# First guess of the norm roots on ScalarE, with the activation tables requested ahead

## The chip, the cores and the metric

One core of one Trainium2 chip runs the whole program. The metric is device microseconds of one execution, as the median of the runs shown.

## The reference, cut to what matters

Four layers work on 256 latent and 256 context tokens of width 1024 (512 columns). Layers 0 and 3 mix tokens by windowed attention with grouped keys, layer 1 by latent attention (MLA), layer 2 by a gated linear recurrence; each is followed by a gated MLP with a short convolution. Norms stand everywhere:

```python
def rmsnorm(x, gain):
    y = x * lax.rsqrt(jnp.mean(x * x, axis=-1, keepdims=True) + EPS)
    return y * gain

for layer in range(DEPTH):
    h = modulate(rmsnorm(x, norm1[layer]), sh1, sc1)      # latent, and context in the same way
    x = x + g1 * mixer(h)       # queries and keys: rmsnorm per head; MLA: also its two low-rank vectors
    x = x + g2 * conv_ffn(modulate(rmsnorm(x, norm2[layer]), sh2, sc2))
```

The root 1 / sqrt(mean + EPS) is what the change computes in another way.

## The kernel before, in words

The residual stream X lies transposed in SBUF: eight tiles of 128 features by 512 tokens, columns 0 to 255 context and 256 to 511 latent. Weights come in units of 128 x 1024 floats (`load`, L215), are split by ScalarE into a rounded high part (`convert`, L222) and by GpSimd into the rest (L226), and every product of a weight matrix takes three matmuls (`mm3`, L235 to L237).

A residual norm is the class `Norm`. `squares` (L434, L436) squares X on ScalarE and sums the tiles on VectorE; `rsq` (L444) sums over features by matmuls with a column of ones into a bank of PSUM, takes the root there with `psum_rsqrt` (L292 to L299), and spreads it over the features with four matmuls (L448); `apply` (L458 to L465) writes the high and low parts of the normed tile. There are 15 such roots, of 128 x 2 values each: two in front of layer 0, two in each of the other six tails of a mixer or MLP that serve both streams, and one in the last layer, whose context half isn't needed. In a tail (`out_tail`) the context half of the last columns is finished first, and the root of the context runs while TensorE goes on with latent columns.

The roots of heads use `mean_rsqrt` (L286, then `rsqrt`, L276 to L281) on small SBUF tiles: one for the keys of each window-attention layer (L643), one for each of 12 blocks of queries (`q_post`, L690, with a scale at L691), two for the low-rank vectors of MLA (L840), two for its first group of heads (L972, L978) and twelve for the later groups (L990). Keys are multiplied by their root (L650, L883, L884), some rotated (L617, L622), copied (L655), and transposed on TensorE (L660, L888); in MLA the query root is folded into the scale of the scores (L920).

So `rsqrt` is twelve VectorE instructions one behind the other: mean plus epsilon, shift and subtract for the integer guess, and three Newton steps of three. `psum_rsqrt` is thirteen, with the guess in PSUM.

A framework traces the program, plans each engine's order of instructions from priorities (program order) and modelled durations, and places the semaphores; `tc.issue_after(x)` keeps what is traced inside it behind x on the same engine. Each engine then runs its own list in order. ScalarE's tables are loaded in sets; before, every load is placed where a function is missing from the set that is loaded. Silu (L185, L1197, L1224), Exp (L1002, L716, L727, L948, L1084), Sqrt (L1088) and Gelu (L1119) need sets; Copy, Identity and Square run under any.

Of the kernel before, what the change touches and what calls it, by code (L numbers as in the profile page):

```python
# [10 lines left out]
F32 = mybir.dt.float32  # L11
F32R = mybir.dt.float32r
BF16 = mybir.dt.bfloat16
I32 = mybir.dt.int32
AF = mybir.ActivationFunctionType
ALU = mybir.AluOpType
# [18 lines left out]
MAGIC = float(0x5F3759DF)  # L35
# [76 lines left out]
def hybrid_kernel(ctx: ExitStack, tc: tile.TileContext, xT, cc, ccT, W, modwa, modwb, modw, colv, rowv, tabs, band, out, depth=DEPTH, dbg=None):  # L112
# [67 lines left out]
    ones = const.tile([128, 1], F32, name="ones")  # L180
    condT = const.tile([128, KT, 32], F32, name="condT")
# [3 lines left out]
    nc.scalar.activation(condT, condT, AF.Silu)  # L185
# [25 lines left out]
    ident = tab("ident")  # L211
    def load(key):
        off, w = offs[key]
        raw = raw_p.tile([128, 1024], F32, tag="raw", name="raw")[:, :w]
        nc.sync.dma_start(raw, bass.AP(tensor=W.tensor, offset=W.offset + off, ap=[[w, 128], [1, w]]))  # L215
        return raw
# [55 lines left out]
    def rsqrt(v, n, steps=3):  # L272
        i = small(n, "rs_i", I32)
        y = small(n, "rs_y")
        t = small(n, "rs_t")
        nc.vector.tensor_scalar(i, v.bitcast(I32), 1, None, op0=ALU.logical_shift_right)  # L276
        nc.vector.tensor_scalar(y.bitcast(I32), i, -1.0, MAGIC, op0=ALU.mult, op1=ALU.add)
        for _ in range(steps):
            nc.vector.tensor_tensor(t, y, y, op=ALU.mult)
            nc.vector.scalar_tensor_tensor(t, t, -0.5, v, op0=ALU.mult, op1=ALU.mult)  # L280
            nc.vector.scalar_tensor_tensor(y, t, 1.5, y, op0=ALU.add, op1=ALU.mult)  # L281
        return y

    def mean_rsqrt(src, n, dim):
        v = small(n, "rs_v")
        nc.vector.tensor_scalar(v, src, 1.0 / dim, EPS, op0=ALU.mult, op1=ALU.add)  # L286
        return rsqrt(v, n)

    def psum_rsqrt(ps, n, dim):
        src, v2, i, y = (ps[:, a * n:(a + 1) * n] for a in range(4))  # L290
        v, t, r = small(n, "rs_v"), small(n, "rs_t"), small(n, "rs_y")
        nc.vector.tensor_scalar(v2, src, 1.0 / dim, EPS, op0=ALU.mult, op1=ALU.add)  # L292
        nc.vector.tensor_scalar(i.bitcast(I32), v2.bitcast(I32), 1, None, op0=ALU.logical_shift_right)
        nc.vector.tensor_scalar(y.bitcast(I32), i.bitcast(I32), -1.0, MAGIC, op0=ALU.mult, op1=ALU.add)
        nc.vector.tensor_scalar(v, src, 1.0 / dim, EPS, op0=ALU.mult, op1=ALU.add)
        for z in range(3):
            nc.vector.tensor_tensor(t, y, v, op=ALU.mult)
            nc.vector.scalar_tensor_tensor(t, t, -0.5, y, op0=ALU.mult, op1=ALU.mult)
            nc.vector.scalar_tensor_tensor(r if z == 2 else y, t, 1.5, y, op0=ALU.add, op1=ALU.mult)  # L299
        return r  # L300
# [109 lines left out]
    class Norm:  # L410
# [28 lines left out]
        def rsq(self, sums):  # L439
# [5 lines left out]
            rs = psum_rsqrt(ps, 2, D)  # L445
# [131 lines left out]
    def swa(l, i, q0, nm, nxt, first=None):  # L577
# [65 lines left out]
        rk = mean_rsqrt(ssk, 16, 64)  # L643
# [21 lines left out]
        def q_post(p, b, ps):  # L665
# [24 lines left out]
            rq = mean_rsqrt(ss, 8, 64)  # L690
            nc.vector.tensor_scalar(rqs[p][:, b * 8:(b + 1) * 8], rq, 0.125, None, op0=ALU.mult)  # L691
# [92 lines left out]
    def mla(l, nm, nxt):  # L784
# [16 lines left out]
        for c, w, ks in ((0, 288, (3, 3, 2)), (1, 384, (2, 2, 2, 2))):  # L801
# [38 lines left out]
            nc.vector.tensor_copy(rrs[c], mean_rsqrt(ss, 4, (256, 384)[c]))  # L840
# [131 lines left out]
        rk = mean_rsqrt(ss, 16, 96)  # L972
# [5 lines left out]
        q_scale(0, 0, 4, mean_rsqrt(ss, 16, 96))  # L978
        units = {}
        for hg in range(4):  # L980
            if hg < 3:
                group(hg + 1)
            for h in range(4):
                core(hg, h // 2, h % 2)
                core(hg, h // 2, 2 + h % 2)
                for b in MP[h] if hg < 3 else ():
# [3 lines left out]
                    rr = mean_rsqrt(ss, 8, 96)  # L990
# [30 lines left out]
    def lru(l, nm, nxt, rates):  # L1021
# [89 lines left out]
        def gelus(n, root):  # L1111
# [5 lines left out]
            with tc.issue_after(root):  # L1117
                for z in range(2):
                    nc.scalar.activation(gg[n][z], gps[2 * n + z], AF.Gelu_apprx_tanh)  # L1119
# [28 lines left out]
        gelus(3, roots[3])  # L1148
# [4 lines left out]
    def ffn(l, t0, nm, nxt):  # L1153
# [26 lines left out]
        def up(f, gh, gl, q):  # L1180
# [16 lines left out]
            nc.scalar.activation(y[:, t0:], y[:, t0:], AF.Silu)  # L1197
# [45 lines left out]

    nm = Norm(0, 0, 0)
# [173 lines left out]
```

## Time and profile before

| | us |
|---|---|
| median of 3 runs | 2228.76 (2225.44 to 2229.73) |
| the profiled execution | 2225.85 |
| its span, first to last instruction | 2224.0 |
| mean granted TensorE clock | 0.983 of full speed |
| table loads in the profile | 20 |

The rows name engines as PE (TensorE matmuls), PEld (its weight loads), DVE (VectorE), ACT (ScalarE), POOL (GpSimd) and SP (the queue that issues transfers). Times count from the first instruction. L and a number is a line of the kernel. Line 269 and line 270 are a helper that splits a tile into high and low part.

### The profile page before, as it was taken

What the parts mean: (1) busy time and instruction counts of PE and PEld (TensorE: products, weight loads), DVE (VectorE), ACT (ScalarE), POOL (GpSimd) and SP (SyncE); (2) the same over time, 40 slices, a digit from 0 to 9 for tenths busy, and PEclk for the clock granted to TensorE, in tenths of its full rate; (3) what the DMA queues carried; (4) which work ended last, traced back from release to release, by engine and by line L of the source; (5) the groups of instructions that cost most, each with busy time, mean ns of one, the idle gap of its engine ahead of it and who ended that gap; (6) DMA issues with size and microseconds to landing.
All of it is one profiled execution on the core that took longest, in us unless ns stands there. A gap on an engine that the chain in (4) does not pass through costs nothing.

```text
span 2224.0 us, 32888 instructions
## 1 busy us (share of the span) xinstructions
PE 2122.6 (95%) x12084; PEld 1764.6 (79%) x12084; DVE 1549.0 (70%) x3341; ACT 1037.4 (47%) x1860; POOL 1050.3 (47%) x760
## 2 busy tenths in 40 slices
PE   6999999999999999999999999889999999898999
PEld 4666888888888666878888887678888888678999
DVE  4677779777776886687888677857954456785333
ACT  4467553232346775532233376824332324675544
POOL 3331255544544113455455457654544444526887
PEclk9999999999999999999999999999999999999999
DMA  7534145554532011255555422224655552313665
GB/s 300 199 127 131 39 135 179 172 178 157 180 114 68 21 30 55 60 190 178 174 186 181 132 67 87 94 88 131 194 184 163 177 163 86 105 33 114 187 182 160
DMA packets 83888, 300.14 MB, mean 135 GB/s; under 512 B 11152, under 2 KB 12816, under 8 KB 81296
## 3 DMA queue, kind: packets, MB, share of 16 engines
q1 hardware_dynamic: 83728, 298.05, 41.9%
q8 instruction: 95, 1.56, 0.3%
q14 instruction: 65, 0.53, 0.1%
HBM read 296.97 MB, written 1.05 MB: 134 GB/s over the span
## 4 chain that ended last, share of the span: by engine, by line
PE 78%; DVE 13%; ACT 4%; DMA 2%; issue 1%; POOL 1%; SPq 0%; ACTq 0%; DVEq 0%
PE fl L235 8%; PE fl L236 8%; PE fl L237 8%; PE mm L236 7%; PE mm L237 7%; PE mm L235 7%; PE mo L235 4%; PE mo L236 4%; PE mo L237 4%; PE tp L235 3%; PE tp L236 3%; PE tp L237 3%; PE mo L751 2%; PE mm L938 2%; PE tp L745 2%
## 5 line engine op out<-in xcount | busy, mean ns | idle before, releaser
L226 POOL TENSOR_TENSOR wlo<-raw,whi 128x256 fp32r<-128x256 f32 (+3 forms) x709 | 1015.6, 1455 | 1106.4 <-ACT whi L222 1068.9
L222 ACT ACTIVATE whi<-raw 128x1024 fp32r<-128x1024 f32 (+3 forms) x367 | 382.5, 1043 | 493.0 <-PE tp L236 208.0
L397 DVE SCALAR_TENSOR_TENSOR junk<-mw,cbc 128x1024 bf16<-128x1024 f32 x256 | 463.8, 1812 | 28.6 <-DMA mw<-in_modw_dram 15.0
L237 PE MATMUL fl<-h_hi,wlo 128*128 128x512 f32 (+1 forms) x800 | 287.1, 359 | 0.1
L235 PE MATMUL fl<-h_hi,whi 128*128 128x512 f32 (+1 forms) x800 | 286.7, 358 | 0.0
L236 PE MATMUL fl<-h_lo,whi 128*128 128x512 f32 (+1 forms) x800 | 286.3, 358 | 0.0
L236 PE MATMUL mm<-h_lo,whi 128*128 128x512 f32 (+1 forms) x784 | 274.6, 352 | 2.5 <-POOL h_lo L463 1.1
L235 PE MATMUL mm<-h_hi,whi 128*128 128x512 f32 (+1 forms) x784 | 273.3, 350 | 2.5 <-ACT h_hi L459 2.5
L237 PE MATMUL mm<-h_hi,wlo 128*128 128x512 f32 (+1 forms) x784 | 273.1, 349 | 0.0
L1193 DVE SCALAR_TENSOR_TENSOR conv<-mm,colt,conv 128x510 f32<-128x510 f32 (+1 forms) x88 | 59.8, 679 | 188.9 <-ACT conv L1191 188.9
L1197 ACT ACTIVATE conv<-conv 128x512 f32<-128x512 f32 (+1 forms) x88 | 51.0, 580 | 291.1 <-DVE conv L1195 291.0
L237 PEld LDWEIGHTS fl<-h_hi,wlo 128*128 128x128 f32 x800 | 151.3, 189 | 23.2 <-POOL wlo L226 1.4
L236 PEld LDWEIGHTS fl<-h_lo,whi 128*128 128x128 f32 x800 | 151.3, 189 | 21.7
L235 PEld LDWEIGHTS fl<-h_hi,whi 128*128 128x128 f32 x800 | 151.5, 189 | 21.5
L236 PEld LDWEIGHTS mm<-h_lo,whi 128*128 128x128 f32 x784 | 148.2, 189 | 24.6 <-DVE h_lo L465 2.9
L235 PEld LDWEIGHTS mm<-h_hi,whi 128*128 128x128 f32 x784 | 148.6, 190 | 22.2 <-ACT h_hi L459 3.5
L237 PEld LDWEIGHTS mm<-h_hi,wlo 128*128 128x128 f32 x784 | 148.3, 189 | 18.8
L235 PE MATMUL mo<-g_hi,whi 128*128 128x512 f32 (+1 forms) x388 | 135.0, 348 | 8.3 <-DVE x L471 8.2
L471 DVE SCALAR_TENSOR_TENSOR x<-mo,modc,x 128x256 f32<-128x256 f32 x193 | 86.5, 476 | 76.5 <-PE mo L237 76.4
L237 PE MATMUL mo<-g_hi,wlo 128*128 128x512 f32 (+1 forms) x388 | 134.8, 347 | 0.0
L236 PE MATMUL mo<-g_lo,whi 128*128 128x512 f32 (+1 forms) x388 | 134.7, 347 | 0.0
L235 PE MATMUL tp<-g_hi,whi 128*128 128x512 f32 (+1 forms) x352 | 124.7, 354 | 0.0
(356 smaller groups left out, 4452.8 us busy)
## 6 DMA issues: line engine op xcount, KB each, us to landing
raw<-in_W_dram SPq DMA_DIRECT2D x352, 512.0 KB, 3.6
mw<-in_modw_dram SPq DMA_DIRECT2D x144, 512.0 KB, 4.2
mw<-in_modwa_dram SPq DMA_DIRECT2D x8, 1024.0 KB, 16.0
mw<-in_modwb_dram SPq DMA_DIRECT2D x16, 512.0 KB, 4.5
mw<-in_modwb_dram SPq DMA_DIRECT2D x8, 1024.0 KB, 9.4
cbc<-in_cc_dram SPq DMA_DIRECT2D x3, 1024.0 KB, 6.7
raw<-in_W_dram SPq DMA_DIRECT2D x8, 384.0 KB, 3.1
x<-in_xT_dram SPq DMA_DIRECT2D x8, 256.0 KB, 4.1
```

Source lines behind the costliest of these rows:

```text
L222: nc.scalar.activation(hi, raw, AF.Copy)
L226: nc.gpsimd.tensor_tensor(lo[:, cs], raw[:, cs], f32(hi[:, cs]), op=ALU.subtract)
L235: nc.tensor.matmul(ps, ah, bh, start=start and i == 0, stop=False, **kw)
L236: nc.tensor.matmul(ps, ah, bl, start=False, stop=False, **kw)
L237: op = nc.tensor.matmul(ps, al, bh, start=False, stop=stop and i == n - 1, **kw)
L397: nc.vector.scalar_tensor_tensor(junk, raw, 1.0, cbc[:, s], op0=ALU.mult, op1=ALU.mult, accum_out=modc[l][:, s, m:m + 1])
L471: nc.vector.scalar_tensor_tensor(X[m][:, half], ps[:, half], modc[l][:, s, part + m:part + m + 1], X[m][:, half], op0=ALU.mult, op1=ALU.add)
L745: nc.tensor.transpose(pp[:, c:c + 128], P[z][:, (2 * kp + kk) * 128:(2 * kp + kk + 1) * 128], ident)
L751: nc.tensor.matmul(po[r], v[0][:, kb, p * 128 + 64 * z:p * 128 + 64 * z + 64], pt[:, kp, (kk * 2 + z) * 128:(kk * 2 + z + 1) * 128], start ...
L938: nc.tensor.matmul(ps[:, c], d["q"][:96, 2 * hp + z, bc], d["k"][:96, 2 * hp + z, :nk], start=True, stop=True)
L1193: op = nc.vector.scalar_tensor_tensor(y3[:, :, 1:], g3[:, :, :255], cw[:, l, 0, f:f + 1], y3[:, :, 1:], op0=ALU.mult, op1=ALU.add)
L1197: nc.scalar.activation(y[:, t0:], y[:, t0:], AF.Silu)
```

## The change

The integer guess goes, and so do two of the three Newton steps. ScalarE computes e = Ln(c * (sum / dim + EPS)) with c = 2^-44, and y = Exp(-e / 2 + ln(c) / 2), which is the first guess; one Newton step follows on VectorE. Constants for the two biases lie in a small tile `seed`. For the queries of window attention the factor of an eighth goes into the second bias, so that the separate scale (L691) falls away, as does the copy of L840. One set holds both Ln and Exp; it is requested by an instruction of its own behind the first Silu of the program, behind the last Silu of each MLP but the final one, and behind the last Gelu of the recurrence, and Ln and Exp are kept behind that request.

```diff
@@ -32,7 +32,7 @@
 MP = ((), (0,), (1,), (2, 3))
 PP0, PP3 = (2, 4, 6), (2, 4, 6)
 QP0, QP3 = (0, 0, 1, 2), (0, 1)
-MAGIC = float(0x5F3759DF)
+LN_C = 2.0 ** -44
 
 
 def unit_plan():
@@ -178,11 +178,15 @@
     rowt = const.tile([128, NROWS], F32, name="rowt")
     tabt = const.tile([128, NTABS], F32, name="tabt")
     ones = const.tile([128, 1], F32, name="ones")
+    seed = const.tile([128, 3], F32, name="seed")
+    tables = [None]
+    for c, value in enumerate((LN_C * EPS, 0.5 * np.log(LN_C), 0.5 * np.log(LN_C) - np.log(8.0))):
+        nc.vector.memset(seed[:, c:c + 1], float(value))
     condT = const.tile([128, KT, 32], F32, name="condT")
     nc.gpsimd.memset(condT, 0.0)
     for j in range(2):
         nc.sync.dma_start(condT[:, :, j], ccT[j])
-    nc.scalar.activation(condT, condT, AF.Silu)
+    silu = nc.scalar.activation(condT, condT, AF.Silu)
     for j in range(KT):
         nc.sync.dma_start(X[j], xT[j])
     nc.sync.dma_start(tabt, tabs)
@@ -269,34 +274,22 @@
         nc.scalar.activation(hi, src, AF.Copy)
         nc.vector.tensor_tensor(lo, src, f32(hi), op=ALU.subtract)
 
-    def rsqrt(v, n, steps=3):
-        i = small(n, "rs_i", I32)
-        y = small(n, "rs_y")
-        t = small(n, "rs_t")
-        nc.vector.tensor_scalar(i, v.bitcast(I32), 1, None, op0=ALU.logical_shift_right)
-        nc.vector.tensor_scalar(y.bitcast(I32), i, -1.0, MAGIC, op0=ALU.mult, op1=ALU.add)
-        for _ in range(steps):
-            nc.vector.tensor_tensor(t, y, y, op=ALU.mult)
-            nc.vector.scalar_tensor_tensor(t, t, -0.5, v, op0=ALU.mult, op1=ALU.mult)
-            nc.vector.scalar_tensor_tensor(y, t, 1.5, y, op0=ALU.add, op1=ALU.mult)
-        return y
-
-    def mean_rsqrt(src, n, dim):
-        v = small(n, "rs_v")
-        nc.vector.tensor_scalar(v, src, 1.0 / dim, EPS, op0=ALU.mult, op1=ALU.add)
-        return rsqrt(v, n)
-
-    def psum_rsqrt(ps, n, dim):
-        src, v2, i, y = (ps[:, a * n:(a + 1) * n] for a in range(4))
-        v, t, r = small(n, "rs_v"), small(n, "rs_t"), small(n, "rs_y")
-        nc.vector.tensor_scalar(v2, src, 1.0 / dim, EPS, op0=ALU.mult, op1=ALU.add)
-        nc.vector.tensor_scalar(i.bitcast(I32), v2.bitcast(I32), 1, None, op0=ALU.logical_shift_right)
-        nc.vector.tensor_scalar(y.bitcast(I32), i.bitcast(I32), -1.0, MAGIC, op0=ALU.mult, op1=ALU.add)
-        nc.vector.tensor_scalar(v, src, 1.0 / dim, EPS, op0=ALU.mult, op1=ALU.add)
-        for z in range(3):
-            nc.vector.tensor_tensor(t, y, v, op=ALU.mult)
-            nc.vector.scalar_tensor_tensor(t, t, -0.5, y, op0=ALU.mult, op1=ALU.mult)
-            nc.vector.scalar_tensor_tensor(r if z == 2 else y, t, 1.5, y, op0=ALU.add, op1=ALU.mult)
+    def log_exp_set():
+        tables[0] = nc.scalar.preload_act_table_set("natural_log_exp_and_others").ins
+
+    def root(src, n, dim, out=None, y=None, eighth=False):
+        if y is None:
+            y = small(n, "rs_y")
+        e, v, t = small(n, "rs_e"), small(n, "rs_v"), small(n, "rs_t")
+        s = 64.0 if eighth else 1.0
+        with tc.issue_after(tables[0]):
+            nc.scalar.activation(e, src, AF.Ln, scale=LN_C / dim, bias=seed[:, 0:1])
+            nc.scalar.activation(y, e, AF.Exp, scale=-0.5, bias=seed[:, 2:3] if eighth else seed[:, 1:2])
+        nc.vector.tensor_scalar(v, src, s / dim, s * EPS, op0=ALU.mult, op1=ALU.add)
+        nc.vector.tensor_tensor(t, y, v, op=ALU.mult)
+        nc.vector.scalar_tensor_tensor(t, t, -0.5, y, op0=ALU.mult, op1=ALU.mult)
+        r = small(n, "rs_r") if out is None else out
+        nc.vector.scalar_tensor_tensor(r, t, 1.5, y, op0=ALU.add, op1=ALU.mult)
         return r
 
     modc = [const.tile([128, 2, 48], F32, name=f"modc{l}") for l in range(DEPTH)]
@@ -442,7 +435,7 @@
             for b in range(2):
                 for z, a in enumerate((acc, sq)):
                     nc.tensor.matmul(ps[:, b:b + 1], a[:, b * 128:(b + 1) * 128], ones, start=z == 0, stop=z == 1)
-            rs = psum_rsqrt(ps, 2, D)
+            rs = root(ps[:, 0:2], 2, D, y=ps[:, 2:4])
             rb = ps[:, 256:]
             for b in range(2):
                 nc.tensor.matmul(rb[:, b * 128:(b + 1) * 128], rs[:, b:b + 1].to_broadcast([128, 128]), ident, start=True, stop=True)
@@ -640,7 +633,7 @@
             sq = tmp("sq")[:, :256]
             nc.scalar.activation(sq, kb, AF.Square)
             nc.vector.tensor_reduce(ssk[:, b * 4:(b + 1) * 4], sq.rearrange("p (h d) -> p h d", d=64), axis=AX.X, op=ALU.add)
-        rk = mean_rsqrt(ssk, 16, 64)
+        rk = root(ssk, 16, 64)
         kh, kl = big("k_hi"), big("k_lo")
 
         krs = []
@@ -687,8 +680,7 @@
                     nc.scalar.activation(qb[:, z], pq, AF.Copy)
                 else:
                     nc.vector.tensor_copy(qb[:, z], pq)
-            rq = mean_rsqrt(ss, 8, 64)
-            nc.vector.tensor_scalar(rqs[p][:, b * 8:(b + 1) * 8], rq, 0.125, None, op0=ALU.mult)
+            root(ss, 8, 64, rqs[p][:, b * 8:(b + 1) * 8], eighth=True)
 
         def scores(ps, p, b, j, g, nk):
             h = 2 * j + g
@@ -837,7 +829,7 @@
                 nc.scalar.activation(sq[:, :(256, 384)[c]], dn[:, b, :(256, 384)[c]], AF.Square, accum_out=ss[:, b:b + 1])
                 if c == 0:
                     nc.scalar.activation(sq[:, :32], dn[:, b, 256:288], AF.Square, accum_out=ssr[:, b:b + 1])
-            nc.vector.tensor_copy(rrs[c], mean_rsqrt(ss, 4, (256, 384)[c]))
+            root(ss, 4, (256, 384)[c], rrs[c])
             if c == 1:
                 continue
             for b in range(4):
@@ -969,13 +961,13 @@
         group(0)
         ss = small(16, "ssk")
         kbs = [kv_mm(0, b, ss[:, b * 4:(b + 1) * 4]) for b in range(4)]
-        rk = mean_rsqrt(ss, 16, 96)
+        rk = root(ss, 16, 96)
         for b in range(4):
             kv_put(0, b, kbs[b], rk[:, b * 4:(b + 1) * 4])
         ss = small(16, "ssq")
         for b in range(4):
             q_mm(0, b, ss[:, b * 4:(b + 1) * 4])
-        q_scale(0, 0, 4, mean_rsqrt(ss, 16, 96))
+        q_scale(0, 0, 4, root(ss, 16, 96))
         units = {}
         for hg in range(4):
             if hg < 3:
@@ -987,7 +979,7 @@
                     ss = small(8, "ss")
                     kb = kv_mm(hg + 1, b, ss[:, 0:4])
                     q_mm(hg + 1, b, ss[:, 4:8])
-                    rr = mean_rsqrt(ss, 8, 96)
+                    rr = root(ss, 8, 96)
                     kv_put(hg + 1, b, kb, rr[:, 0:4])
                     q_scale(hg + 1, b, 1, rr[:, 4:8])
                 if hg == 3:
@@ -1116,7 +1108,8 @@
                 gg[n] = tmp("gg"), tmp("gg")
             with tc.issue_after(root):
                 for z in range(2):
-                    nc.scalar.activation(gg[n][z], gps[2 * n + z], AF.Gelu_apprx_tanh)
+                    op = nc.scalar.activation(gg[n][z], gps[2 * n + z], AF.Gelu_apprx_tanh)
+            return op.ins
 
         def merge(n):
             if n % 2 == 0:
@@ -1145,7 +1138,9 @@
         merge(1)
         gelus(2, roots[3])
         merge(2)
-        gelus(3, roots[3])
+        last = gelus(3, roots[3])
+        with tc.issue_after(last):
+            log_exp_set()
         merge(3)
         out_tail(l, 16, [("lwo", m) for m in range(KT)], 1, tiles(rh[0], rl[0]) + tiles(rh[1], rl[1]), 0, nxt, tail_ps,
                  None, (mm_ps, mm_ps, tp_ps), 2)
@@ -1194,7 +1189,10 @@
                                                 op0=ALU.mult, op1=ALU.add)
             nc.vector.scalar_tensor_tensor(y3[:, :, :255], g3[:, :, 1:], cw[:, l, 2, f:f + 1], y3[:, :, :255],
                                            op0=ALU.mult, op1=ALU.add)
-            nc.scalar.activation(y[:, t0:], y[:, t0:], AF.Silu)
+            silu = nc.scalar.activation(y[:, t0:], y[:, t0:], AF.Silu)
+            if f == NF - 1 and l < depth - 1:
+                with tc.issue_after(silu.ins):
+                    log_exp_set()
             nc.vector.tensor_tensor(pv[:, t0:], y[:, t0:], pv[:, t0:], op=ALU.mult)
             split(gh[:, q, t0:], gl[:, q, t0:], pv[:, t0:])
             return op.ins
@@ -1241,6 +1239,8 @@
                 for j in range(KT):
                     nc.sync.dma_start(out[j], X[j][:, NCTX:])
 
+    with tc.issue_after(silu.ins):
+        log_exp_set()
     nm = Norm(0, 0, 0)
     rbs = [nm.stats(s) for s in (1, 0)]
     nm.tiles()
```

## Rows read from the trace of the kernel before

**Rows 1.** The page's busy table: us, share of the span, instructions.

```profile
PE 2122.6 (95%) x12084; PEld 1764.6 (79%) x12084; DVE 1549.0 (70%) x3341; ACT 1037.4 (47%) x1860; POOL 1050.3 (47%) x760
```

**Rows 2.** List of waits, whole span: us in total, times, longest us.

```profile
ACT g_hi L269 <- DVE fl L1198: 58.5, 42, 2.0
...
PE tp L448 <- DVE rs_y L299: 6.8, 7, 2.6
PE tp L660 <- ACT P L655: 6.7, 2, 4.2
PE tp L745 <- DVE P L737: 6.4, 5, 2.7
...
PE tp L888 <- DVE rqs L920: 5.8, 2, 3.8
...
PE tp L888 <- DVE kn L884: 4.4, 2, 2.3
...
PE tp L888 <- DVE st L949: 1.6, 2, 1.4
```

**Rows 3.** Timeline of DVE, layer 3's key root: start, us, instruction, count.

```profile
1900.29 0.18 DVE L286 TENSOR_SCALAR rs_v<-ssk 128x16 f32<-128x16 f32 x1
...
1905.77 0.65 DVE L280 SCALAR_TENSOR_TENSOR rs_t<-rs_t,rs_v 128x16 f32<-128x16 f32 x1
1906.45 0.17 DVE L281 SCALAR_TENSOR_TENSOR rs_y<-rs_t,rs_y 128x16 f32<-128x16 f32 x1
```

**Rows 4.** Timeline of PE; in brackets the idle time before and its releaser.

```profile
17.89 1.23 PE L448 MATMUL tp<-tabt,rs_y 128*128 128x128 f32 x4 [2.48 <-DVE rs_y L299]
...
718.02 0.50 PE L235 MATMUL fl<-whi,ck_hl 128*128 128x512 f32 x1 [1.26 <-DVE qn L904]
...
1908.47 0.69 PE L660 MATMUL tp<-tabt,P 128*128 128x128 f32 x2 [4.23 <-ACT P L655]
```

**Rows 5.** Windows over seven root spans (last, sum): PE, PEld, DVE, ACT, POOL busy.

```profile
1900.20:1906.60 6.40, 4.04 (x18) 3.00 (x16) 5.99 (x13) 1.61 (x2) 5.56 (x8) 0.99 0.36 116
sum 35.30, PE 27.39 PEld 21.41 DVE 32.30 ACT 17.99 POOL 21.56; mean PE 3.91 PEld 3.06 DVE 4.61 ACT 2.57 POOL 3.08
```

**Rows 6.** Timeline of DVE, last layer's residual root: first and last of thirteen.

```profile
2023.91 0.17 DVE L292 TENSOR_SCALAR tp<-tp 128x2 f32<-128x2 f32 x1 [2.01 <-PE tp L444]
...
2026.27 0.16 DVE L299 SCALAR_TENSOR_TENSOR rs_y<-rs_t,tp 128x2 f32<-128x2 f32 x1
```

**Rows 7.** ACT by line and shape: busy us, mean ns, idle before.

```profile
L222 ACT ACTIVATE whi<-raw 128x1024 fp32r<-128x1024 f32 x352 | 371.1, 1056 | 487.0 <-PE tp L236 208.0 <-PE mm L236 181.8 <-PE fl L237 23.7
...
L459 ACT ACTIVATE h_hi<-hn,modc 128x256 fp32r<-128x256 f32 x120 | 55.5, 501 | 47.8 <-DVE hn L458 47.6
...
L434 ACT ACTIVATE sq<-x 128x256 f32<-128x256 f32 x49 | 19.8, 410 | 31.7 <-DVE x L471 31.7
...
L730 ACT ACTIVATE st<-st 128x2 f32<-128x2 f32 x48 | 9.4, 196 | 0.2
```

**Rows 8.** Windows behind three of the seven waits; third from the end: granted clock.

```profile
754.60:758.00 3.40, 2.76 (x14) 2.14 (x15) 2.73 (x8) 1.48 (x3) 2.32 (x5) 1.00 0.72 220
...
799.20:803.00 3.80, 3.80 (x17) 3.12 (x18) 3.70 (x12) 1.01 (x2) 1.41 (x3) 0.68 0.56 177
...
1908.40:1913.50 5.10, 5.03 (x16) 4.03 (x17) 2.88 (x8) 2.75 (x5) 3.33 (x4) 0.52 0.17 66
```

**Rows 9.** Timeline of ACT, latent attention's first softmax and the recurrence's end.

```profile
717.40 1.28 ACT L948 ACT_TABLE_LOAD   x1
718.91 0.56 ACT L948 ACTIVATE P<-mm,st,rqs 128x256 f32<-128x256 f32 x1 [0.23 <-DVE st L946]
...
1451.88 0.63 ACT L269 ACTIVATE r_hi<-gg 128x512 fp32r<-128x512 f32 x1 [7.48 <-DVE gg L1127]
```

**Rows 10.** Window of latent attention, columns as in rows 5.

```profile
700.00:890.00 190.00, 175.28 (x1098) 127.14 (x1098) 148.48 (x517) 126.97 (x305) 36.08 (x54) 0.97 0.13 38
```

**Rows 11.** List of waits, weight loads of PE behind copied probabilities.

```profile
PEld mo L965 <- ACT pt L253: 15.7, 33, 0.8
```

## The prediction

> **What bounds the kernel now.** I read the page's busy table first: TensorE (PE) works for 2122.6 of 2224.0 us [rows 1]. So PE is the bound in most places, and a change to small work of VectorE (DVE) pays only where PE stands still for it. The list of waits says where. Seven times PE waits for transposes (of rotated keys in window attention, of keys in latent attention) whose input hangs on a norm root: 6.7 + 5.8 + 4.4 + 1.4 = 18.3 us. The roots of the residual norms cost it 6.8, and the probabilities that DVE scales 6.4 [rows 2]. The timeline shows the worst of the seven: the keys' sums are ready at 1900.25, the root's twelve DVE instructions run from 1900.29 to 1906.62 [rows 3], and PE idles 4.23 us before 1908.47 [rows 4]. Twelve instructions of 0.17, 0.21 from start to start, would be 2.5 us; most of these take 0.65 to 0.68, because GpSimd (POOL) is subtracting weights beside them: POOL is busy 5.56 of those 6.40 us, and 21.56 of 35.30 in the seven spans together [rows 5]. Where no POOL piece disturbs, thirteen instructions take 2.52 us, 0.19 each from start to start [rows 6].
>
> **What a root becomes.** There are 45 roots: 15 of residual norms (13 DVE instructions each) and 30 in the attentions (12, and 13 or so where a scale or copy follows). Each becomes Ln and Exp on ScalarE (ACT), three dependent DVE instructions, and one that forms v beside ACT. ACT's smallest instruction takes 0.196; a bias read from a tile adds 501 - 410 = 91 ns [rows 7], so I put Ln or Exp at 0.285, the pair at 0.57. The three DVE instructions are 3 x 0.21 = 0.6 undisturbed and 3 x 0.69 = 2.1 under POOL. Ln may also stand behind one weight conversion, up to 1.06 [rows 7]. A new root is thus 1.2 to 3.7 us, against 2.5 undisturbed and 3.2 to 6.9 in the seven places.
>
> **A, the seven waits.** Taking each with what ACT and POOL do there: the first (4.6 us, conversion half done, POOL running) saves 1.4; 699.8 (4.4) 1.5; 748.7 and 757.6, where ACT is free and POOL mostly silent, all of their PE waits, 2.1 and 1.4; 790.4 all 2.1; 837.5 (5.7) 2.6; 1900.2 (6.4) 3.2. Sum 14.3. The keys' other inputs and PE's fixed order come next, so I count two thirds: **-9.5**, bounds 0 and -18.3.
>
> **B, the clock behind them.** After five of the seven waits PE runs 3.1 to 5.1 us at a granted clock of 0.50 to 0.68, at or partly at the lower level of 1.2 GHz; after the wait of 2.12 at 754.6 it stays at 1.00 [rows 8], where two of the five and that one stand. Length times lost clock is 1.2 and 2.4 in those two, 8.6 in the five. With waits cut to about 1 us most of this should vanish: **-5**, bounds 0 and -8.6.
>
> **C, the start.** PE waits 2.48 before 17.89 [rows 4] for the first root. DVE and ACT are free, so the chain of 3.7 falls to about 1.3, but what PE multiplies next, the first modulation weights, may not have landed by then: **-1.5**, bounds 0 and -2.5.
>
> **D, the residual norms.** In the last layer 2.52 us of DVE [rows 6] lie bare in PE's longest wait for a norm, 2.6 [rows 2]; 0.57 + 0.6 replace them: -1.3. The roots in the other layers' tails share the remaining 6.8 - 2.6 - 2.5 = 1.7 [rows 2], since PE has latent columns to go on with: -1.7. Together **-3**, bounds 0 and -4.3.
>
> **E, tables.** Loads move. In latent attention the exponential's load at 717.40 takes 1.28 [rows 9], and beside it PE waits 1.26 at 718.02 behind the interleaved root [rows 4]; asked for at the end of the feed-forward, the load is gone there: **-1.3**, bounds 0 and -1.5. The new places are covered: at the end of the feed-forward the load stands behind Silu, where ACT waits for DVE's product anyway (58.5 us in 42 waits, 1.4 each [rows 2]); in the recurrence it stands behind the last Gelu, after which ACT idles 7.48 us before r_hi [rows 9]. Without cover each of the first is 1.28 on ACT, with most of a layer's matrix work still to run. The recurrent layer pays two loads more, 2.6 us if that cover were gone; I count 0. The row has 1.28 and nothing behind it: the load ends at 718.68 and the next activation starts at 718.91, on a DVE input. The Trainium skill speaks against such moves ("ScalarE: Activation LUTs", What ACT_TABLE_LOAD costs: a drain of about 1380 ns with each load, 2.66 us a switch); by it the two extra loads would be 5.3 us uncovered. No drain shows in this trace, so the sum stays with 1.28.
>
> **F, DVE's queue in window attention.** Twelve query roots leave nine DVE instructions fewer each in front of the probabilities, for which PE waits 6.4 [rows 2]: **-2**, bounds 0 and -6.4.
>
> **G, ACT's queue.** The 30 attention roots add 60 x 0.285 = 17 us to ACT. It is busy 126.97 of 190 us in latent attention [rows 10], and PE already waits 15.7 us, 33 times, for its copies of the transposed probabilities [rows 11]. Ln and Exp also stand in order: until the reduction before Ln is done, conversions, copies and exponentials behind it wait, and with them POOL and PE. A third of the 17 falls where it is needed: **+6**, bounds 0 (its idle third takes all) and +17.
>
> Sum: -9.5 - 5 - 1.5 - 3 - 1.3 - 2 + 6 = -16.3. The profiled execution took 2225.85 us (span 2224.0), 2.9 under the median of the runs shown, 2228.76, and inside their 2225.44 to 2229.73. So 2209.6, and I say **2210**.
>
> **Rivals.** (1) *Given back.* The keys' multiplications, rotations and copies follow the root on DVE and ACT, and PE's instructions stand in an order written ahead; each wait closed opens the next one a microsecond later. Then A is a quarter (-3.5), B -1, C to F half (-4), G +6: -2.5, or 2223. For it: PE does not start its transposes until 1.8 us after the root of 1906.62. Against: that rest is the same before and after, so what the root loses should come through. (2) *ACT becomes late*, slower than before: Ln, at the head of ACT's line, waits for its sum while the copy of the transposed probabilities that PE wants stands behind it. Price: 0.57 plus some 0.5 of standing for each of 30 roots, 32 us, of which 60% lands on PE's waits for ACT: +19. With C and D kept (-4.5) and a third of A and B (-5) that is about +10, 2236. It decides when a root holds ACT up by more than the 2 us that its place gains, or when ACT is above nine tenths busy there; now it is two thirds [rows 10]. (3) *The tables don't stay.* If each exponential of the softmax fetched another set than the root's, every attention root would cost two loads: 60 x 1.28 = 77, some 2290. Against it, the trace has one load for many exponentials, and the new set holds both functions. (4) *All of it*: A to F at full bounds near -40, G half: 2193.
>
> **How the numbers follow.** The forecast holds 0.70, given back 0.15, ACT late 0.10, tables 0.02, all of it 0.03. What a measurement of this kernel can tell from no change is about 0.2%, 4.5 us. The forecast's own range is 2195 to 2222; taking in rival 1 and unfortunate terms of G, 2195 to 2230 leaves out about 2 in 10. Faster by over 0.2%: 0.74 (forecast, rival 4, a bit of rival 1); within: 0.14; slower: 0.12. The order in which the framework plans each engine's instructions may shift with the durations, for some microseconds either way; the range has room for it.
>
> **What would show it.** Right: the seven waits of PE for key transposes add up to under 9 us, PE's clock after them stays near 1.00, the last norm's wait is near 1.3, the load inside latent attention is gone, DVE has some 390 instructions fewer. Wrong: waits of the same size with another releaser (rival 1); waits for ACT's copies above 25 us or ACT standing on Ln (rival 2); more than some 25 table loads (rival 3).

## The result and the profile after

The changed kernel takes 2202.74 us (median of four runs, 2198.82 to 2209.43); the kernel before, timed with it, 2227.48 (2225.44 to 2229.73). The ratio is 0.9884 [0.9871, 0.9898]: 24.7 us faster, where 16.3 were forecast, and inside the range. The profiled execution of the changed kernel took 2199.70 us, span 2197.9.

The page's busy table of the changed kernel, which answers to [rows 1]:

```profile
PE 2112.3 (96%) x12084; PEld 1756.3 (80%) x12084; DVE 1487.3 (68%) x2955; ACT 1056.5 (48%) x1952; POOL 1050.0 (48%) x760
```

Two numbers are worth keeping from such a line: the span less TensorE's (PE) busy time, which is the time PE stands idle, and the busy time itself, which for the same matmuls follows the clock that the chip grants (in the fourteen profiles of this case it lies between 2112.0 and 2151.3 us, and times the clock of that run between 2084 and 2093). Idle: 2224.0 - 2122.6 = 101.4 before, 2197.9 - 2112.3 = 85.6 after, so 15.8 us fewer. Busy: 10.3 us fewer, with the same 12084 matmuls. Together they are the 26.1 us between the two profiled spans. A second profile of the changed kernel, the run e9 below, has an idle time of 85.9. VectorE (DVE) issues 386 instructions fewer and ScalarE (ACT) 92 more.

The list of waits of the changed kernel, answering to [rows 2] and [rows 11]:

```profile
PEld mo L957 <- ACT pt L258: 13.9, 32, 0.9
...
DVE rs_t L289 <- ACT rs_y L287: 6.8, 10, 1.0
...
PE tp L653 <- ACT P L648: 5.2, 3, 2.8
...
PE fl L241 <- POOL wlo L231: 2.3, 3, 1.0
...
PE tp L880 <- DVE st L938: 2.1, 1, 2.1
...
PE tp L441 <- DVE rs_r L292: 1.9, 2, 1.4
...
PE tp L880 <- DVE kn L876: 1.5, 1, 1.5
...
PE tp L880 <- DVE rqs L912: 0.6, 1, 0.6
```

L653, L880 and L441 are the old L660, L888 and L448. The waits for key transposes, 18.3 us in seven, are now 9.4 in six (1.81, 1.53, 0.64, 2.10, 2.82 and 0.54 in PE's timeline). Those for the norms' broadcast fell from 6.8 to 1.9, and the copies of the transposed probabilities (L957, before L965) hold up PE's weight loads no longer than before (13.9 against 15.7). The line of POOL's weight pieces (wlo, waited for by matmuls into fl) has no counterpart in the list of before.

The worst of the seven, layer 3's key root, in the timelines of DVE and then of PE after; they answer to [rows 3] and [rows 4]:

```profile
1882.12 0.17 DVE L288 TENSOR_SCALAR rs_v<-ssk 128x16 f32<-128x16 f32 x1
1883.15 0.28 DVE L289 TENSOR_TENSOR rs_t<-rs_y,rs_v 128x16 f32<-128x16 f32 x1 [0.85 <-ACT rs_y L287]
1883.47 0.66 DVE L290 SCALAR_TENSOR_TENSOR rs_t<-rs_t,rs_y 128x16 f32<-128x16 f32 x1
1884.16 0.67 DVE L292 SCALAR_TENSOR_TENSOR rs_r<-rs_t,rs_y 128x16 f32<-128x16 f32 x1
1884.87 1.77 DVE L643 TENSOR_TENSOR kraw<-kraw,rs_r 128x256 f32<-128x256 f32 x2
1886.56 1.81 DVE L610 TENSOR_TENSOR kr<-kraw,rowt 128x256 f32<-128x256 f32 x2
```

```profile
1888.22 0.44 PE L653 MATMUL tp<-tabt,P 128*128 128x128 f32 x2 [2.82 <-ACT P L648]
...
1999.75 0.58 PE L441 MATMUL tp<-tabt,rs_r 128*128 128x128 f32 x1 [1.42 <-DVE rs_r L292]
```

The root lasts 2.71 us instead of 6.33, but PE's wait behind it falls only from 4.23 to 2.82. In both kernels GpSimd (POOL) starts eight weight pieces about 0.6 us after the keys' sums are ready. Before, they lay beside the root; now the root is over sooner, and they lie beside its last steps and what follows it. POOL's timeline before and after, and the same multiplication and rotation in the timeline of DVE before:

```profile
1900.83 5.56 POOL L226 TENSOR_TENSOR wlo<-raw,whi 128x256 fp32r<-128x256 f32 x8 [2.91 <-ACT whi L222]
```

```profile
1882.66 6.30 POOL L231 TENSOR_TENSOR wlo<-raw,whi 128x256 fp32r<-128x256 f32 x8 [2.91 <-ACT whi L227]
```

```profile
1906.66 0.76 DVE L650 TENSOR_TENSOR kraw<-kraw,rs_y 128x256 f32<-128x256 f32 x2
1907.34 0.75 DVE L617 TENSOR_TENSOR kr<-kraw,rowt 128x256 f32<-128x256 f32 x2
```

The four instructions take 1.51 us before, with POOL silent, and 3.58 after, with five POOL pieces beside them. Here the rival "given back" is at work, for 2 of 3.6 us.

The clock behind the waits: windows of the changed kernel (columns as in [rows 5]; third from the end the granted clock), answering to [rows 8]:

```profile
840.30:844.30 4.00, 3.97 (x18) 2.67 (x19) 2.85 (x9) 1.97 (x6) 0.00 (x0) 1.00 0.44 131
1888.20:1893.20 5.00, 4.42 (x21) 2.96 (x22) 3.90 (x9) 2.96 (x4) 2.99 (x4) 1.00 0.37 116
1999.70:2004.70 5.00, 3.84 (x16) 3.55 (x17) 3.69 (x10) 2.92 (x7) 0.74 (x1) 0.50 0.36 105
```

Behind five of the key waits, these two among them, the clock stays at 1.00. Behind the last norm it is 0.50, as it was before. One execution is not enough to tell where the clock comes back: in the second profile of the same kernel (e9) PE waits the same 2.82 us before 1888.07, and the window behind it is at 0.58:

```profile
1888.00:1892.00 4.00, 3.93 (x13) 3.22 (x14) 3.53 (x9) 2.10 (x4) 1.12 (x2) 0.58 0.37 139
```

In the recurrent layer, which has no attention root, the second norm's windows went from 0.77 in the kernel before (first fence) to 1.00 (second):

```profile
1499.80:1507.30 7.50, 6.54 (x37) 6.04 (x38) 6.45 (x21) 4.82 (x12) 4.39 (x6) 0.77 0.42 141
```

```profile
1489.40:1496.90 7.50, 7.25 (x57) 6.85 (x58) 6.40 (x18) 6.04 (x16) 5.54 (x8) 1.00 0.43 137
```

### The profile page after: what moved, and what is told of

It is laid out like the page before. It is cut to its first block, busy times and chain, and to the rows that moved or that the text cites. A ratio compares the mean times of both kernels' runs of the same rounds, so it can differ in the third digit from the quotient of the medians.

```text
span 2197.9 us, 32610 instructions
## 1 busy us (share of the span) xinstructions
PE 2112.3 (96%) x12084; PEld 1756.3 (80%) x12084; DVE 1487.3 (68%) x2955; ACT 1056.5 (48%) x1952; POOL 1050.0 (48%) x760
## 4 chain that ended last, share of the span: by engine, by line
PE 82%; DVE 9%; ACT 3%; DMA 2%; POOL 2%; issue 2%; SPq 0%; ACTq 0%; DVEq 0%; POOLq 0%
PE fl L242 9%; PE fl L240 9%; PE fl L241 9%; PE mm L242 7%; PE mm L241 7%; PE mm L240 7%; PE mo L240 4%; PE mo L241 4%; PE mo L242 4%; PE tp L240 3%; PE tp L241 3%; PE tp L242 3%; PE mo L743 2%; POOL wlo L231 2%; PE mm L930 2%
```

## Experiments

All are edits of the changed kernel unless another is named. Idle is span less PE busy of the profiled execution, clock the mean granted clock of all runs of a kernel.

```
kernel            median us  ratio to before         span    idle   clock
before            2227.48    1                       2224.0  101.4  0.983
after             2202.74    0.9884 [.9871, .9898]   2197.9   85.6  0.987
e1_residual       2213.42    0.9946 [.9927, .9965]   2209.7   95.9  0.986
e2_attention      2210.87    0.9935 [.9914, .9956]   2208.8   93.3  0.988
e3_three_steps    2216.64    0.9957 [.9941, .9973]   2215.2   94.8  0.986
e4_dve_one_step   2204.21    0.9905 [.9883, .9927]   2203.7   85.7  0.985
e5_no_request     2291.73    1.0295 [1.0281, 1.0309] 2291.0  139.7  0.973
e6_no_newton      2198.67    0.9868 [.9851, .9885]   2198.9   82.7  0.986
e7_left_out       2196.31    0.9866 [.9852, .9879]   2193.5   79.3  0.986
e8_late_request   2204.91    0.9912 [.9899, .9926]   2208.5   85.6  0.985
e9_after_again    2202.84    0.9900 [.9877, .9923]   2197.9   85.9  0.988
e10_extra_acts    2210.49    0.9934 [.9914, .9954]   2205.1   90.7  0.988
e11_v_first       2199.06    0.9879 [.9855, .9903]   2200.1   87.9  0.990
e12_mixed         2193.38    0.9845 [.9832, .9859]   2196.3   79.9  0.988
```

**Residual roots alone, attention roots alone.**

```diff
# e1: the attention roots are the old ones
-        rk = root(ssk, 16, 64)
+        rk = mean_rsqrt(ssk, 16, 64)
...
# e2: the residual roots are the old ones
-            rs = root(ps[:, 0:2], 2, D, y=ps[:, 2:4])
+            rs = psum_rsqrt(ps, 2, D)
```

> The changed kernel with only the 15 residual-norm roots changed; the 30 attention roots go back to the integer guess and three steps on VectorE; tables are requested as in the change. Theory (the attention roots bring most of the gain, through PE's seven waits and the clock behind them): about 8 us faster than the kernel before, ratio 0.9965. Rival (the residual roots bring most): 18 us, 0.992. Rival (any change of durations replans the order, and the gain comes from that): 20 us or more whatever part is taken, 0.991.

> Only the 30 attention roots changed; the residual norms keep the root of thirteen VectorE instructions; tables as in the change. Theory: about 17 us faster than before, ratio 0.9925, with PE's waits for key transposes at 9 us as in the changed kernel. Rival (residual roots): 8 us, 0.9965. Rival (replanned order): 20 us or more, 0.991.

The residual roots bring 0.54%, the attention roots 0.65%, and 0.54 + 0.65 = 1.19 agrees with the whole's 1.16, each within some 0.2. In idle time it is 5.5 and 8.1 of 15.8. By time the residual share came out between the two expectations, 11.5 us; half of it is no idle time and goes with the clock, for its idle time is near the forecast's C and D (4.5). Each part closes its own waits: with the residual roots alone the waits for key transposes stay at 18.3 us and those for the norms' broadcast fall to 1.9, with the attention roots alone they are 8.8 and 6.4.

**Three Newton steps, and one step without ScalarE.**

```diff
# e3: the new first guess, then
+        for z in range(3):
...
# e4, on the kernel before
-    def rsqrt(v, n, steps=3):
+    def rsqrt(v, n, steps=1):
...
-        for z in range(3):
+        for z in (2,):
```

> The changed kernel with three Newton steps instead of one behind the ScalarE guess: six more VectorE instructions in each root. Theory (the length of the chain on VectorE beside GpSimd is what counts): six instructions of 0.21 to 0.69 us are 1.3 to 4.1 us a root, and about half of the gain goes, 13 us faster than before, ratio 0.994, with the waits for key transposes back near 15 us. Rival (VectorE's share of the guess, the table moves or the order make the gain): stays within 4 us of the changed kernel, 0.9885.

> The kernel before with one Newton step in place of three, all on VectorE, tables untouched (its root is a coarser approximation: two of three steps are left out). Theory as forecast (ScalarE's queue costs 6 us): the short chain without ScalarE is faster than the changed kernel by that, less the 1.3 us of the table load, about 29 us faster than before, ratio 0.987. Rival (ScalarE's part is free): as the changed kernel or a little slower, 22 to 25 us faster, 0.989 to 0.990. Rival (the gain is in the tables and in moving work off VectorE): under 12 us, 0.995.

With three steps behind the new guess, 9.2 of the 15.8 us of idle time are gone again, and about two thirds of the gain in time. With the old integer guess and one step, all on DVE and with two of three steps left out, the idle time is that of the changed kernel (85.7 against 85.6), and the 29 us that I drew from the forecast's price for ScalarE did not come: 20.7 by the medians. So saving two steps is enough for the whole gain in idle time, and ScalarE's pair costs no more there than the two instructions of the old guess; the logarithm's part is to be a guess good enough to save the steps. The two kernels don't add up, though: with all three steps behind the new guess 6.6 us of the gain are left, and no run tells which of the other edits (the guess off DVE, v formed beside ACT, the tables, the order) brings them.

**The requests for tables.**

```diff
# e5: no requests
-        tables[0] = nc.scalar.preload_act_table_set("natural_log_exp_and_others").ins
+        pass
...
# e8: requests behind the context half's last Square
+            if s and self.ask:
+                with tc.issue_after(op.ins):
+                    log_exp_set()
```

> The changed kernel without its five requests for tables, nothing else: each function then brings its own table when its turn comes. Theory (the tables are what makes the change pay): Ln and Exp then fetch a table each, two loads of 1.28 us in every root, 45 roots, 115 us more on ScalarE; about 15 to 20 of the roots have TensorE waiting at their end, so 40 to 50 us more on the path, with clock lost behind the longer waits: 2240 to 2275, ratio to the kernel before 1.007 to 1.022, slower than before. Rival 1 (one set holds both and the loads are few anyway): within 0.3% of the changed kernel, ratio 0.987 to 0.992. Rival 2 (the loads also split the softmax's exponentials and all 115 us land on the path): above 2300, ratio above 1.035.

> The changed kernel with four of its five requests moved from behind the last Silu or Gelu to behind the last Square of the next norm's context half, so that the load stands between the Squares and the logarithm. Theory (asking ahead matters only where ScalarE is on the path): TensorE's two sums and the latent half's matmuls stand between Square and Ln and hide 1.28 us in part; 0 to +3 us, ratio 0.988 to 0.990. Rival (the load ahead is what pays): 1.28 us each on the path with the clock behind it, +5 to +9 us, ratio 0.990 to 0.993.

Without requests nearly every root fetches twice. The loads by line, and ACT's timeline at a key root in latent attention, of the kernel without requests:

```profile
L285 ACT ACT_TABLE_LOAD x45 | 57.7, 1283 | 0.8
L286 ACT ACT_TABLE_LOAD x43 | 55.2, 1283 | 0.8
```

```profile
720.36 1.28 ACT L285 ACT_TABLE_LOAD   x1
721.65 0.31 ACT L285 ACTIVATE rs_e<-ssk,seed 128x16 f32<-128x16 f32 x1
721.98 1.28 ACT L286 ACT_TABLE_LOAD   x1
723.27 0.31 ACT L286 ACTIVATE rs_y<-rs_e,seed 128x16 f32<-128x16 f32 x1
```

88 loads are 112.9 us of ACT, and the time rises by 2291.73 - 2202.84 = 88.9: more than I expected, and within 2 us of what the forecast's rival on the tables gave, from another number of loads. 54 us of it are idle time of PE; the rest is mostly clock, which falls to 0.973. ACT's busy time rose by 110.2 against the changed kernel, with 84 loads more in all (106 against 22). The loads start within 0.02 us behind the instruction ahead of them, and 84 of the 88 end 0.01 us before their activation starts. The Trainium skill ("ScalarE: Activation LUTs", What ACT_TABLE_LOAD costs) adds a drain of 1380 ns to each switch; an estimate from its figure, 88 x 2.66, is 234 us on ACT. No run here shows the drain.

Asked for late, the load costs no idle time (85.6 again). The median is 2.1 us above the changed kernel's beside a lower clock, and the two intervals overlap, though the ratio lies in the rival's range. That the set is asked for pays; whether it pays to ask before the Squares rather than behind them stays open within these 2 us.

**Without the Newton step, and without the root.**

```diff
# e6
-        nc.vector.tensor_scalar(v, src, s / dim, s * EPS, op0=ALU.mult, op1=ALU.add)
-        nc.vector.tensor_tensor(t, y, v, op=ALU.mult)
...
-        return r
+        return y
# e7, in place of Ln, Exp and the step
+        nc.vector.tensor_scalar(r, src, 0.0, 0.03 if eighth else 0.25, op0=ALU.mult, op1=ALU.add)
```

> The changed kernel with the exponential's output taken as the root: the one Newton step and its four VectorE instructions are left out of all 45 roots. Theory (what the chain of a root lasts lands on TensorE's waits, at the residual norms nearly in full, and the clock behind them follows): three chained VectorE instructions of 0.15 to 0.38 us fewer in each root, about 0.6 us at each of some 20 waits, 8 to 12 us with the clock: 2191 to 2196, ratio 0.984 to 0.987. Rival 1 (the change already took all that the roots had to give, what waits is the rotation and the copies behind them): 0 to -3 us, ratio 0.987 to 0.990. Rival 2 (VectorE free earlier, its queue is the gain, as the forecast's small term for the queue had it): 155 instructions fewer, -2 to -4 us.

> The floor: each of the 45 roots is one VectorE instruction that writes a constant; Ln, Exp and the Newton step are left out, tables are still asked for. Theory (chain length lands on TensorE's waits): against the changed kernel two activations of 0.26 to 0.30 us and three VectorE steps fewer in each chain, 1.2 to 1.8 us at some 20 waits, half or more of it on the path: -12 to -20 us, 2183 to 2191, ratio 0.980 to 0.984. Rival (the forecast's rest, the idle time of TensorE that is left belongs to other waits): -2 to -6 us, ratio 0.985 to 0.988. If ScalarE's part of the change had a price of its own (the +6 of the forecast), this kernel gains more than the one without the Newton step by over 6 us.

The floor, a constant in place of the root, has 79.3 us of idle time, so by this measure all the roots together cost PE 101.4 - 79.3 = 22.1 us of idle time before and 6.3 after. The change has taken 15.8 of 22.1, and I had expected two to three times as much to be left. By the ratio the rival's numbers hold: my expectation charged chain length to some 20 waits, and after the change the root decides few of them. Nor does the kernel without any pair on ScalarE gain 6 us over the one without the step (2.4 by the medians), as it should if the pair had the forecast's price. Leaving the step out saves 2.9 us of idle time. By stages it saves in latent attention (idle 13.8 to 10.0) and in the last layer's front (14.0 to 12.2), and loses in the first layer (29.1 to 32.3). For scale: the same stage of the same kernel, latent attention, has 13.8 in one profile and 15.4 in the other.

**The queue of ScalarE, and the scatter of the runs.**

```diff
# e10, behind the pair, in the 30 attention roots
+                for _ in range(2):
+                    xe, xy = small(n, "rs_xe"), small(n, "rs_xy")
+                    nc.scalar.activation(xe, src, AF.Ln, scale=LN_C / dim, bias=seed[:, 0:1])
+                    nc.scalar.activation(xy, xe, AF.Exp, scale=-0.5, bias=seed[:, 1:2])
```

> The changed kernel with the logarithm and the exponential of each of the 30 attention roots issued twice more behind the first pair, into tiles that nobody reads: 120 activations of 0.30 us more, 36 us on ScalarE, at the place where the change put its pair. The forecast charged +6 us (0 to 17) for one such pair in each root, so by it two pairs more are +12 (0 to 34): 2212 to 2218. Rival, to which the runs so far point (ScalarE has room at these places, the pair costs nothing in the queue): 0 to +3 us against the changed kernel, idle time of TensorE within 2 us of its 85.6.

> The changed kernel as it is, timed beside the two below and in as many rounds as they are, since its four runs spread over 10 us. Theory (its idle time of TensorE is fixed, 16 us below that of before, and the spread of one kernel's runs is the granted clock behind the waits): 2200 to 2206, ratio 0.988 to 0.991, and the longer runs show the lower clock. Rival (part of the gain was a happy clock of the first four runs): 2206 to 2212.

The page of the kernel with the extra pairs, and its list of waits:

```profile
PE 2114.4 (96%) x12084; PEld 1754.6 (80%) x12084; DVE 1493.5 (68%) x2955; ACT 1081.5 (49%) x2072; POOL 1048.4 (48%) x760
```

```profile
PEld mo L962 <- ACT pt L258: 12.5, 30, 0.9
...
PE fl L240 <- ACT rs_xe L291: 3.0, 2, 1.8
```

One of these two waits in the timeline of PE, and DVE just ahead of it:

```profile
751.30 0.41 PE L240 MATMUL fl<-whi,cq_hi 128*128 128x384 f32 x1 [1.77 <-ACT rs_xe L291]
```

```profile
750.61 0.55 DVE L905 TENSOR_TENSOR qn<-fl,mcq 128x384 f32<-128x384 f32 x1
```

Two pairs more cost 4.8 us of idle time (90.7 - 85.9) and 7.7 of the median: neither the +12 of the forecast's price nor nothing. The copied probabilities are waited for no longer (12.5). The list names an extra Ln as the releaser of two new waits (3.0 us), but PE's matmul reads nothing of it: it writes fl anew, which DVE reads until 751.16, 0.06 us before that Ln ends. Which of the two holds PE is not shown. Both waits lie in latent attention, where I had seen the danger, and there the idle time is 13.9 (300.22 less 286.32 in a window over the stage) beside the 15.4 of the same stage in e9; the price falls in the two window attentions (32.2 against 28.7 and 16.4 against 13.4). If one pair costs half of two, which no run shows, it costs 2.4 us by idle time and 3.9 by the medians.

The kernel run again gives 2202.84 and the same idle time, so the first four runs were not lucky.

**One line moved, and two edits put together.**

```diff
# e11
+        nc.vector.tensor_scalar(v, src, s / dim, s * EPS, op0=ALU.mult, op1=ALU.add)
         with tc.issue_after(tables[0]):
...
# e12: e11, and in the attention roots
+        if not newton:
+            return y
```

> The changed kernel with one line moved: v, the scaled sum for the Newton step, is written ahead of the logarithm instead of behind the exponential. In the trace of the change, at the residual norms v waits for the exponential though it reads the sums alone, and stands in the chain with 0.16 us and its handover. Theory: 0.2 us less in each of 15 residual roots, up to 3 us if each lands, some 2 us: 0 to -3 us against the changed kernel, the last norm's wait of 1.42 us falls to about 1.2. Rival (the order of the other instructions shifts and gives it back): within 1 us, with the last norm's wait shorter all the same.

The theory fell. The last norm's root in the changed kernel (DVE) and with v first (ACT):

```profile
1998.96 0.16 DVE L288 TENSOR_SCALAR rs_v<-tp 128x2 f32<-128x2 f32 x1 [2.63 <-ACT tp L287]
```

```profile
2001.07 0.26 ACT L287 ACTIVATE rs_e<-tp,seed 128x2 f32<-128x2 f32 x1 [1.11 <-DVE rs_v L285]
```

Written last, v waits for the exponential, which writes its guess into the same tile (tp) that holds the sums; written first, it is waited for by the logarithm, though both only read the sums. So v keeps its place in the chain, and the wait is 1.51 instead of 1.42. The tile lies in PSUM. The Trainium skill ("PSUM — Partial Sum Buffer", PSUM bank collisions raise a hardware error) has it that two engines may not touch one bank's quadrant at once, reads included, and that the software orders them; the two timelines agree. The shorter median stands beside a higher clock and 2.3 us more idle time, so it is not a gain that I can explain.

> The two variants that came out under the changed kernel put together: the 15 residual roots keep the Newton step with v written first, the 30 attention roots take the exponential's output as the root (their Newton step is left out). Theory (each edit shortens other chains, and TensorE's idle time adds up: with no Newton step at all the two attention stages in the middle and at the end lost 5.6 us of idle time, while the residual stages gained nothing): idle time 78 to 82 us, 2194 to 2199, ratio 0.985 to 0.988. Rival (the order of the instructions decides at this size, not the chains): 2198 to 2204, idle time 82 to 87 us.

The mixed kernel, whose attention roots lack the Newton step and are coarser for it, has 79.9 us of idle time, as the theory had it, and 2193.38 us, just under its range. Its ratio 0.9845 [0.9832, 0.9859] lies clear of the changed kernel's, 0.9900 [0.9877, 0.9923] when run again: it beats both kernels, by about 0.5% the changed one.

## Why the prediction was right, and where its sizes were off

**A held in its waits, less so in idle time.** The seven waits gave 18.3 - 9.4 = 8.9 us, forecast 9.5; the mark "under 9 left" was missed by 0.4 (in the second profile 8.8 are left). The two thirds that I counted are an average: three of the waits fell to nothing, as forecast (5.6 us), and the other four gave 3.3 of the 8.7 that I had listed for them. In layer 3 the reason was the one given, the keys' other work took back 2 of 3.6 us. But not all of it reached the idle time. Windows over latent attention, before, after, and after run again (span of the stage, then PE busy):

```profile
632.18:942.23 310.05, 292.33 (x1905) 236.84 (x1905) 225.27 (x736) 195.23 (x457) 91.58 (x124) 0.98 0.17 49
```

```profile
627.28:931.12 303.84, 290.01 (x1901) 233.49 (x1901) 200.94 (x570) 201.55 (x496) 91.84 (x124) 0.98 0.16 50
```

```profile
626.30:928.12 301.82, 286.39 (x1901) 229.67 (x1901) 200.90 (x570) 201.41 (x496) 91.73 (x124) 1.00 0.16 50
```

The key waits of this stage fell from 11.6 to 4.3 us, and the 1.26 of E went too, 8.6 together; the stage's idle time fell from 17.7 to 13.8 and 15.4 only. More than half opened again at other waits: 2.3 us (3.7 in the second profile) for POOL's weight pieces, the rest for copied probabilities, exponentials and small steps of the root. That is what the rival "given back" described, in one stage; as ACT makes the copies and exponentials, a part may be G's.

**C and D held.** The last norm's root lasts 1.34 us instead of 2.52, and the wait fell from 2.60 to 1.42: -1.2, forecast -1.3. The first root's wait fell from 2.48 to 0.45, -2.0 against -1.5:

```profile
17.56 1.22 PE L441 MATMUL tp<-tabt,rs_r 128*128 128x128 f32 x4 [0.45 <-DVE rs_r L292]
```

All waits for the norms' broadcast fell by 4.9, against 4.5 for C and D, and the residual roots alone lowered idle time by 5.5.

**E came true for another reason.** The wait of 1.26 us and the load beside it are both gone, and the loads went from 20 to 22 in all. But e1 has no load there either, with the old attention roots, and its list still has the wait:

```profile
PE fl L241 <- DVE qn L915: 1.3, 1, 1.3
```

So the wait hung on the old root in DVE's queue and not on the load. That the size came out is luck.

**F was mis-sized: -2, measured near -6.** PE's waits for the transposes of the scaled probabilities (L745, now L737) were 6.4 us [rows 2], with four smaller releasers 8.6; now they are 2.8:

```profile
PE tp L745 <- DVE st L726: 1.1, 2, 0.8
...
PE tp L745 <- DVE q L689: 0.5, 1, 0.5
PE tp L745 <- DVE rs_y L281: 0.3, 1, 0.3
...
PE tp L745 <- ACT P L735: 0.3, 1, 0.3
```

```profile
PE tp L737 <- DVE st L721: 0.8, 1, 0.8
...
PE tp L737 <- DVE st L718: 0.7, 2, 0.5
PE tp L737 <- DVE rs_t L289: 0.7, 1, 0.7
...
PE tp L737 <- ACT P L727: 0.4, 1, 0.4
...
PE tp L737 <- DVE P L729: 0.2, 1, 0.2
```

With the attention roots alone they are 2.8 too, with the residual roots alone 7.7. The shorter attention roots were worth nearly the whole of my bound here; whether by DVE's queue, as F had it, or as links of the chain in front of the probabilities, no run separates.

**G was mis-sized: +6, more likely 2 to 4, and not at the place that it named.** Its argument, a third of 17 us falls where it is needed, put the price on the copied probabilities; the weight loads' wait for them did not grow, and PE itself waits 1.2 us for them in latent attention. Below, the price is bounded by nothing (e4, which has no pair on ACT and the same idle time), above by what two more pairs cost, 4.8 us of idle time and 7.7 of the median; 2 to 4 is half of that, an estimate.

Together A, C, D, E and F closed 8.9 + 4.9 + 1.3 + 5.8 = 20.9 us of waits, and the idle time fell by 15.8: the other 5.1 opened elsewhere. G and "given back" are both in these 5.1, and the runs don't divide them. In the forecast the same terms are -17.3 and G's +6, -11.3 together. So the forecast's idle terms were short mainly by F, and its +6 came near the 5.1 by luck, for it stood for one cause of them only.

**B was mis-sized: -5, measured near -8.** I looked for the clock only behind five of the key waits. In the profile it did come back there, to 1.00, but in e9 not behind the worst of them, and it came back elsewhere too. Windows over the recurrent stage, which has residual roots alone, before and after:

```profile
1266.46:1523.00 256.54, 235.49 (x1267) 200.96 (x1266) 186.28 (x288) 153.97 (x231) 156.10 (x159) 0.95 0.26 81
```

```profile
1258.51:1508.22 249.71, 230.44 (x1261) 197.33 (x1260) 180.83 (x252) 157.60 (x241) 156.28 (x159) 0.97 0.27 83
```

Of the 10.3 us of busy time that PE lost in the profiled run, 5.1 lie between these two (some 1 us of it are six matmuls that the second window misses); in e9 the stage has 232.1. Part of that is no effect of a root: behind the recurrence's longest wait, 6.3 us before and 6.1 after, the clock was 0.54 and 0.78. Only the mean over many runs tells the size. It rises from 0.9835 (44 runs of before, beside the experiments) to 0.9873 (nine of after), which on 2122.6 us of busy time is 2122.6 x (1 - 0.9835/0.9873) = 8.2.

So -15.8 of idle time and -8.2 of clock give -24.0, and the runs -24.7; the forecast had -11.3 and -5. Of the rivals, "given back" took a part of the gain, more than half of it in latent attention; "ACT late" is seen at a small fraction of its price; and the tables' price is what the kernel without requests paid.

## What to carry to other kernels

Split a gain into idle time and busy time of the engine that bounds: for the same instructions the first tells what waits did, the second mostly what the clock did; here they are 15.8 and 10.3 us. Add up the waits that closed and hold the sum against the idle time: the difference, here 5.1 us, has opened elsewhere. A floor kernel, with the suspected work replaced by a constant, says what is left to win before the next idea is built; here 6 of 22 us of idle time. What activations cost on an engine that is half idle is found by issuing more of them, not by a share of its busy time.

## What was not expected

The scatter of this kernel's runs is nearly all clock. The 44 runs of the kernel before that stood beside the experiments span 2214.4 to 2233.2 us at mean clocks of 0.988 to 0.980; 0.8% of 2122.6 us of busy time is 17 of these 18.8.

The length of one wait does not tell the clock behind it. After 2.82 us of waiting at 1888.22 the clock was 1.00, and in e9, after the same wait, 0.58; after the last norm's 1.42, with waits of 1.52 and 0.52 in the four us ahead of it, 0.50. Its root was halved and nothing of the clock came back there, in e9 neither.

Of the roots' small DVE instructions in the changed kernel, 40 of the 60 with an operand in PSUM lie wholly beside a POOL piece, and the longest takes 0.160 us. Of the 90 Newton steps that read and write other tiles only, none lies wholly within a POOL piece. The 58 that meet no piece take 0.15 to 0.18 us; of the 32 that do, 31 take 0.28 to 0.75, and each of these ends 0.02 to 0.03 us behind a piece, as if it could not end before. The wide ones behind the key root take about 0.9 instead of 0.4. So a root in PSUM is not slowed by POOL here, and one outside is. The roots in PSUM are also the narrowest, with two columns, but a softmax step of one column on other tiles (L935) takes 0.16 us alone and, in two of three meetings with a piece, 0.63 and 0.64.
